# The even mixer takes RWKV's value columns before the attention's columns

## The chip, the cores and the metric

One Trainium2 chip, one of its cores. The metric is the device time of one launch in microseconds (us). All numbers before the result come from the kernel before the change: three timed runs and one profiled execution. The engines are called PE (TensorE), ACT (ScalarE), DVE (VectorE), POOL (GpSimd) and SP (the queue that loads the weights).

## What is computed

A trunk of two layers over 256 tokens of 1024 features, in float32. Each layer is a macaron: a half-step SwiGLU FFN, a mixer, a second half-step FFN, each with an RMSNorm before and after. The change touches only the mixer of layer 0, the "even" one, which runs two things side by side on the same normed input `h`:

```python
z = h @ w_in                                   # 1536 attention + 1792 RWKV columns
qa, ka, va = split(za)                         # differential attention, 4 heads, 2 x 64 / 128
r, k, v, xw, xa, xg = split(token_shift(zb))   # RWKV-7, 8 heads of 64
oa = softmax(q1 k1) va - lam * softmax(q2 k2) va
state = state * w + (state @ -kk) (kk a) + v k ;  y = state @ r      # token by token
mix = concat(rms_norm(oa), group_norm(y) * g) @ w_out
```

The order in which the columns of `w_in` are multiplied does not matter for the result.

## The kernel before, in words

The 256 tokens are two blocks of 128. All weights stream from HBM once as units of 128 x 2048 values, each loaded in two halves by SP's queue (line 289), and split by ACT (line 299) and DVE (line 300) into two float32r parts. A product with streamed weights is three passes: lines 315 to 317 (`proj`, tokens on the partitions, 12 products of 512 columns a unit and block), lines 340 to 342 (`proj_features`, features on the partitions, both blocks at once, 48 products of 256 columns a unit) and lines 327 to 329 (`outp`, output products, 12 a unit and block). The text calls all of these the wide products. At most 4 units are held split, counted from the slower block (`NW`, line 281).

The even mixer has 17 units: 13 of inputs and 4 of outputs. `EVEN_ORDER` (line 45) says in which order the inputs come: k, r, low-rank, q2, k2, v2 (attention's value), v (RWKV's value). k, r, v2 and v are two units each, q2 and k2 are two units of two heads each, low is one. The function that uses a finished input (`left`, line 859) is called one unit later, for the low-rank inputs and the last entry of the order at once.

Three further lines of work hang on them:

- `low_rank` (line 746) forms RWKV's features and puts `rwkv` (line 1059) of its block on a lane (2 x block). Its steps, each up to a `yield`: `pl`, `pt`, five doublings of the inverse (lines 1107, 1114), `pm` and `po` (lines 1128, 1133); then it waits for RWKV's value (lines 1139, 1140) and, in block 1, for block 0's state (line 1144); then `pr` and `pz` twice (lines 1155 to 1164), in block 0 the state (lines 1173 to 1184), two steps of `pk` and `py` (lines 1192, 1197 to 1200), and the norm with `pg` (line 1222).
- `value` (line 780) forms RWKV's value: scaled by ACT, mixed with the token before by DVE and `pv` on PE (line 785, in block 1 also line 787).
- `attention` (line 935) is put on lane 1 once q2 and k2 are there, block 0 ahead of block 1: scores `sp` (line 950), softmax on DVE and ACT (lines 953 to 972), transposes and weighted sums `op` (lines 983, 989) once v2 is there, norm and two turns (line 349). Block 0 does its four heads at once, block 1 two and two.

The order is set by a planner, `run` (line 1252). Block 0 may be `LAG` = 3 units ahead of block 1, in the units that `LAGS` names only 2. After every unit each lane takes a step (lane 2 slightly more), and when no block can go on, lanes take steps alone:

```python
order = (0, 1) if ready(0) else (1,) if ready(1) else ()
if not order:
    waits = [False, False]
    order = (0, 1) if ready(0) else (1,) if ready(1) else ()
    self.step_lanes()
```

Lanes issue with a lift in priority (`LIFT`, 200 for lane 0, 600 for lanes 1 and 2). From that the framework fixes each engine's order of instructions ahead of time. Transposes, scores, sums and `pv` share two PSUM banks (`tp`).

After the inputs `even` takes four output units, attention's two first and then RWKV's two (line 875); block 0's wait until both blocks are through with the inputs, block 1's until block 0's recurrence is done.

Of the kernel before, what the change touches and what calls it, by code (L numbers as in the profile page):

```python
# [15 lines left out]
PSUM = bass.MemoryType.PSUM  # L16

P = 128
# [7 lines left out]
LAM_INIT = 0.2  # L26
NW = 8  # half units, split
NRAW = 3  # half units, as loaded
LAG = 3
LAG0 = (6, 12)  # L30
WIDE = 16
LAGS = {"even": (7, 10, 2)}
LIFT_PRE, LIFT_POST = 300, 100
# [6 lines left out]

# units of the weight stream, and where each sub-layer starts
U_FFN, U_EVEN, U_ODD = 3 * NCH, 17, 32
# columns of the even mixer's inputs in the order that they are taken: RWKV's k, r, v and
# low-rank inputs, the attention's q2, k2, v2
EVEN_ORDER = ("k", "r", "low", "q2", "k2", "v2", "v")
PLAN = [("ffn", 0, 0), ("even", 0, 0), ("ffn", 0, 1), ("ffn", 1, 0), ("odd", 1, 0), ("ffn", 1, 1)]
SIZES = {"ffn": U_FFN, "even": U_EVEN, "odd": U_ODD}


# ---------------------------------------------------------------- constants of the shapes  # L50
def _columns(spec):
# [13 lines left out]
CO, CO_N = _columns([("dec", 4 * 2 * 128)])  # L65
# per-feature parameters, one feature per partition
PR, PR_N = _columns(
# [45 lines left out]

# ---------------------------------------------------------------- layout of the inputs
def _layout(inputs):
    a = {n: np.asarray(v) for n, v in inputs.items()}
    f = np.float32

    def cols(w, k_tiles=4):
        # [K, n] -> units of k_tiles K-tiles of n columns each  # L120
        k, n = w.shape
        return w.reshape(-1, k_tiles, P, n).transpose(0, 2, 1, 3).reshape(-1, P, k_tiles * n)

    def ffn(l, j, i):
        c0, c1 = JOINT.get(i, JOINT[None])
        w = a["ffn_wgu"][l, j]
        # halves of the inputs with gate and up side by side, or all the inputs of gate and then of up
        solo = w.reshape(2, 4, P, 2, NCH, 256).transpose(4, 0, 2, 1, 3, 5).reshape(NCH, 2, P, 2048)
        both = w.reshape(8, P, 2, NCH, 256).transpose(3, 2, 1, 0, 4).reshape(NCH, 2, P, 2048)
        gu = np.concatenate([solo[:c0], both[c0:c1], solo[c1:]])  # L130
        dn = cols(a["ffn_wd"][l, j], 2)
        out = []
        for c in range(NCH):
            out += [gu[c, 0], gu[c, 1]]
            if c:
                out.append(dn[c - 1])
        return out + [dn[NCH - 1]]
# [33 lines left out]
    units = []  # L171
# [48 lines left out]

# ---------------------------------------------------------------- the kernel
class Trunk:
    def __init__(self, ctx, tc, io, out, plan):
# [13 lines left out]
        nc.scalar.dma_start(out=c0, in_=io["c0"])  # L237
        # what is loaded ahead of which half unit: (block, half of the features)
        self.ahead = {X[0]: [(0, 0)], X[1]: [(0, 1)], X[2]: [(1, 0), (1, 1)]}
        nc.vector.memset(self.mhalf, -0.5)  # L240
        # the parts of the inputs' transposes, [features, block, tokens]
        self.xh = self.sb.tile([P, 8, 2, P], F32R, name="xh")
# [4 lines left out]

        # weight stream
        self.n_units = sum(SIZES[s[0]] for s in plan)
        self.pos = [0, 0]  # L250
        self.raws, self.split, self.n_dma, self.n_split = {}, {}, 0, 0

    # -------- small helpers
    def col(self, name, i=0, rows=P):
# [13 lines left out]
    def ps(self, tag, name="ps"):  # L268
        # two banks for each tag: ac0, ac1 (sums of the blocks), mm, tp
        return self.ps_p.tile([P, 512], F32, tag=tag, name=name)  # L270
# [6 lines left out]

    # -------- weights: load, then split each value exactly into two float32r parts
    def pump(self):
# [23 lines left out]

    # -------- products with the streamed weights (three exact-part passes)
    def proj(self, ps, u, first, last, xT, width=512):
# [25 lines left out]
    def proj_features(self, ps, u):  # L331
        # [2 x 128 features, 256 tokens], of both blocks
        w, xh, xl = self.split[u], self.xh, self.xl
# [10 lines left out]
    def turn(self, b, src, g=None):  # L344
        # [128 tokens, 2, 128] -> parts of its transpose, scaled by feature
        nc = self.nc
# [14 lines left out]

    # -------- norms
    def power(self, v, eps, n=1, name="rs"):
        # (v + eps) ** -0.5
        s = self.small(n, "pw_in")
        r = self.small(n, name, bufs=6)
        self.nc.vector.tensor_scalar(out=s, in0=v, scalar1=eps, scalar2=None, op0=ALU.add)
        self.nc.gpsimd.tensor_tensor(out=r, in0=s, in1=self.mhalf[:, :n], op=ALU.pow)
        return r

    def power2(self, v, eps, name):
        # (v[0] + v[1] + eps) ** -0.5
        s = self.small(1, "ssv")
# [39 lines left out]
    def spread(self, b, rs):  # L413
        # 1 / rms of the inputs along the free dimension
        rw = self.t2("rw")[:, :P]
# [36 lines left out]

    # -------- SwiGLU
    def ffn(self, b, u, l, j):
        """Hidden features 256 at a time: the first and the last ones block by block, the others for both
        blocks at once, whose products come out with the features on the partitions, as the second
        product takes them."""
        nc = self.nc
# [80 lines left out]

    # -------- retention  # L540
    def odd(self, b, u, l, j):
        """The queries and keys come out with the features on the partitions, for both blocks at once
        and without the norm's factors: the keys' go with the values, the queries' with the head's norm."""
        nc, mx, S = self.nc, self.mix, self.shared
# [124 lines left out]

    # -------- differential attention and RWKV-7 side by side  # L670
    def even(self, b, u, l, j):
# [21 lines left out]
        def last_cols(parts):  # L693
            # columns of equal height together
            at = 0
# [7 lines left out]
        def shifted(parts, name):  # L703
            # parts: (source [p, 128] in PSUM, mu, 1 - mu, destination, slot)
            zm = T2("zm", 516).rearrange("p (a t) -> p a t", a=4)
# [87 lines left out]

        # of both blocks at once, two heads at a time, [features, block, tokens]; the norm's factors
        # go with the keys here and with the scores for the queries
        def keys(i, ps):
# [72 lines left out]

        # the sums take banks that the other block is through with  # L870
        def free():
# [18 lines left out]
    def even_setup(self):  # L890
# [9 lines left out]
        self.row(S["muv"], R_MUV, 512, nc.sync)  # L900
        # 1 - mu, and the two coefficients of 1 + (a - 1) k_a in terms of tanh
        om = mx.tile([P, 20], F32, name="om")
# [14 lines left out]
        S["sub"] = sub  # L917
        # -lambda on every partition
        lv = self.t2("lv")[:, :256]
# [15 lines left out]
    def attention(self, b, qT, kT, rs):  # L935
        nc, mx, S = self.nc, self.mix, self.shared
        V, A, mm = nc.vector, nc.scalar, nc.tensor.matmul
        n, H = (b + 1) * P, 4 >> b  # keys, and heads at a time
        d0 = CE["dist"][0] + 256 - n
# [63 lines left out]
    def rwkv_features(self, b, fk, fr, th, ta):  # L1003
        """What the recurrence needs of each feature, in the scale of the block's middle."""
        nc, mx, S = self.nc, self.mix, self.shared
# [9 lines left out]
        for g in range(2):  # L1015
# [28 lines left out]
            A.activation(out=kk, in_=kk, func=AF.Square)  # L1044
            # the first two columns of each product count; more cost nothing, and the array's clock
            # does not fall for want of work
            pn = self.tp("pn")[:, : 8 * WIDE].rearrange("p (n i c) -> p n i c", n=2, i=2)
# [11 lines left out]
    def rwkv(self, b, F, sxg):  # L1059
# [7 lines left out]
        else:  # L1067
            # the features of the block are formed: their room serves the recurrence
            ln, nt, xx, yy, pp = (mx.tile([P, 8, 64], F32, tag=t, name="work") for t in ("th", "ta", "fk", "fr", "w"))
        h8 = lambda ap: ap.rearrange("p (h c) -> p h c", c=64)  # L1070
        # two banks, one for each row half of the array: even heads and odd heads
        pair = lambda name, n: [ac(name)[:, : 4 * n].rearrange("p (h c) -> p h c", h=4) for _ in range(2)]
# [7 lines left out]

        # triangular system inside each half block
        pl = pair("pl", 64)
# [16 lines left out]

        # inverse of the system, by doubling the solved blocks  # L1100
        groups = (slice(0, 4), slice(4, 8))
# [35 lines left out]

        # state that the block starts from, in the block's own scale, head by head
        while f"v{b}" not in S:
# [28 lines left out]
        if not b:  # L1168
            # state after the block
            st = mx.tile([P, 4, 64], F32, tag="st", name="st")  # L1170
# [32 lines left out]

        # norm over each head, bonus, gate
        lw, lb = self.t2("lnw"), self.t2("lnb")
# [20 lines left out]

    # -------- run
    def block(self, b):
# [105 lines left out]
```

## Time and profile before

| what | us |
|---|---|
| median of the three timed runs | 1209.59 |
| lowest and highest run | 1209.18, 1213.92 |
| span of the profiled execution, first to last instruction | 1225.8 |
| another time of that execution | none is given beside its span |
| PE busy in it | 1201.0 (98%) |
| DVE busy, ACT busy | 690.7 (56%), 576.1 (47%) |
| mean granted clock of TensorE | 0.979 |

A profile shows one execution, from the first to the last instruction. Busy time of PE is modelled, as matmuls are pipelined, so a full PE is not PE at its peak. The granted clock is a share of the full speed; 0.50 is the lower of two levels (1.2 GHz against 2.4). A float32 product shows as two instructions. An instruction's row gives its start, its length, engine, line, operation, output and inputs, its shape, how many like it follow (x4), and in brackets how long the engine idled before it and what ended that.

### The profile page before, as it was taken

Reading aid. Unit: us, or ns where it says so; the run is one execution under the profiler, and the core shown is the slowest. Engines: PE = TensorE matmul, PEld = TensorE weight load, DVE = VectorE, ACT = ScalarE, POOL = GpSimd, SP = SyncE. Lnnn points to the kernel's source line nnn. Section 1 sums busy time; section 2 is a strip of 40 time slices with the busy share of each in tenths; the row PEclk is TensorE's granted clock in tenths of the full one; section 3 lists DMA queues with packets and bytes.
Section 4 is the critical chain, followed back from the end, with each engine's and each line's share of the span. In section 5 each row is a group of like instructions: output and inputs, shape, how many; then the busy total and the mean of one; then the engine's idle time right before and its main releaser. Section 6 shows DMA issues by size and latency. Waiting matters only on the chain.

```text
span 1225.8 us, 19872 instructions
## 1 busy us (share of the span) xinstructions
PE 1201.0 (98%) x8072; PEld 1050.6 (86%) x8072; DVE 690.7 (56%) x987; ACT 576.1 (47%) x895; POOL 38.9 (3%) x53
## 2 busy tenths in 40 slices
PE   7999999999999999999999999999999999999997
PEld 6999997888778769999978999988987777899996
DVE  5664456787552475554565555565445557555453
ACT  6554446743541264444465444456434456544442
POOL 0000001000011100000010000000000001000000
PEclk9999999999995799999999999999999999999999
DMA  8665556431230056555555655555525555555651
GB/s 277 219 224 176 190 178 192 138 105 61 68 114 1 31 165 214 190 175 188 181 181 172 198 180 194 182 181 191 190 85 180 163 167 188 182 196 184 196 185 39
DMA packets 55419, 199.84 MB, mean 163 GB/s; under 512 B 6176, under 2 KB 6432, under 8 KB 55328
## 3 DMA queue, kind: packets, MB, share of 16 engines
q1 hardware_dynamic: 54576, 196.90, 49.2%
q8 instruction: 63, 1.03, 0.3%
q0 software_dynamic: 320, 1.05, 0.3%
q10 hardware_dynamic: 432, 0.63, 0.2%
q14 instruction: 28, 0.23, 0.1%
HBM read 197.50 MB, written 1.05 MB: 162 GB/s over the span
## 4 chain that ended last, share of the span: by engine, by line
PE 87%; DVE 3%; ACT 3%; DMA 3%; issue 2%; POOL 1%; SPq 0%; DVEq 0%; POOLq 0%; ACTq 0%
PE ps L340 13%; PE ps L342 13%; PE ps L341 13%; PE ps L328 8%; PE ps L327 8%; PE ps L329 8%; PE ps L315 4%; PE ps L317 4%; PE ps L316 4%; DMA raw<-in_wts_dram 2%; ACT wh L299 1%; DVE wl L300 1%; PE pk L1192 1%; PE p L1107 1%; PE p L1114 1%
## 5 line engine op out<-in xcount | busy, mean ns | idle before, releaser
L300 DVE TENSOR_TENSOR wl<-raw,wh 128x1024 fp32r<-128x1024 f32 (+1 forms) x368 | 442.5, 1205 | 378.2 <-ACT wh L299 375.5
L299 ACT CAST wh<-raw 128x1024 fp32r<-128x1024 f32 (+1 forms) x368 | 379.3, 1035 | 446.1 <-PE ps L341 275.7
L340 PE MATMUL ps<-xh,wh 128*128 128x256 f32 x1376 | 390.9, 284 | 1.8 <-DVE sgh L491 1.4
L342 PE MATMUL ps<-xh,wl 128*128 128x256 f32 x1376 | 390.1, 284 | 0.0
L341 PE MATMUL ps<-xl,wh 128*128 128x256 f32 x1376 | 389.4, 283 | 0.0
L340 PEld LDWEIGHTS ps<-xh,wh 128*128 128x128 f32 x1376 | 263.5, 192 | 6.3 <-DVE sgh L491 2.3
L341 PEld LDWEIGHTS ps<-xl,wh 128*128 128x128 f32 x1376 | 263.5, 192 | 1.6
L342 PEld LDWEIGHTS ps<-xh,wl 128*128 128x128 f32 x1376 | 263.6, 192 | 0.5
L328 PE MATMUL ps<-wl,hx 128*128 128x512 f32 x448 | 180.2, 402 | 0.0
L327 PE MATMUL ps<-wh,hx 128*128 128x512 f32 x448 | 178.5, 399 | 0.0
L329 PE MATMUL ps<-wh,hx 128*128 128x512 f32 x448 | 178.1, 398 | 0.0
L315 PE MATMUL ps<-wh,xh 128*128 128x512 f32 (+1 forms) x320 | 129.8, 408 | 2.2 <-ACT xh L401 1.6
L316 PE MATMUL ps<-wl,xh 128*128 128x512 f32 (+1 forms) x320 | 126.6, 398 | 0.0
L317 PE MATMUL ps<-wh,xl 128*128 128x512 f32 (+1 forms) x320 | 125.3, 396 | 0.7 <-DVE xl L402 0.7
L329 PEld LDWEIGHTS ps<-wh,hx 128*128 128x128 f32 x448 | 84.8, 189 | 20.3 <-issue 0.5
L327 PEld LDWEIGHTS ps<-wh,hx 128*128 128x128 f32 x448 | 85.0, 190 | 19.9 <-issue 0.5
L328 PEld LDWEIGHTS ps<-wl,hx 128*128 128x128 f32 x448 | 84.8, 189 | 17.6
L315 PEld LDWEIGHTS ps<-wh,xh 128*128 128x128 f32 x320 | 60.7, 190 | 21.7 <-ACT xh L401 6.7
L317 PEld LDWEIGHTS ps<-wh,xl 128*128 128x128 f32 x320 | 60.6, 189 | 15.5 <-DVE xl L402 2.7
L316 PEld LDWEIGHTS ps<-wl,xh 128*128 128x128 f32 x320 | 60.6, 189 | 12.7 <-issue 1.7
L401 ACT ACTIVATE xh<-tp,c 128x128 fp32r<-128x128 f32 x96 | 32.3, 366 | 11.0 <-PE tp L396 6.5
L402 DVE SCALAR_TENSOR_TENSOR xl<-tp,c,xh 128x128 fp32r<-128x128 f32 x96 | 30.7, 347 | 11.9 <-ACT xh L401 10.3
(233 smaller groups left out, 831.0 us busy)
## 6 DMA issues: line engine op xcount, KB each, us to landing
raw<-in_wts_dram SPq DMA_DIRECT2D x362, 512.0 KB, 4.5
gpost<-in_rows_dram SPq DMA_DIRECT2D x6, 512.0 KB, 5.6
x<-in_x_dram SPq DMA_DIRECT2D x4, 256.0 KB, 6.1
ups<-in_ups_dram SPq DMA_DIRECT2D x1, 768.0 KB, 7.4
ce<-in_ce_dram SPq DMA_DIRECT2D x1, 644.0 KB, 7.3
lnw<-in_rows_dram POOLq DMA_DIRECT2D x2, 256.0 KB, 4.0
lnb<-in_rows_dram POOLq DMA_DIRECT2D x2, 256.0 KB, 3.6
dec<-in_co_dram SPq DMA_DIRECT2D x1, 512.0 KB, 3.4
```

Source lines behind the costliest of these rows:

```text
L299: nc.scalar.copy(out=h[:, c], in_=r[:, c])
L300: nc.vector.tensor_tensor(out=l[:, c], in0=r[:, c], in1=h[:, c].bitcast(F32), op=ALU.subtract)
L315: mm(ps[:, :width], lhsT=xh[:, kt, :], rhs=h[:, c], start=first and i == 0, stop=False)
L316: mm(ps[:, :width], lhsT=xh[:, kt, :], rhs=l[:, c], start=False, stop=False)
L317: mm(ps[:, :width], lhsT=xl[:, kt, :], rhs=h[:, c], start=False, stop=last and i == n - 1)
L327: mm(acc[n], lhsT=hh[:, t], rhs=wh[:, c], start=first and t == 0, stop=False)
L328: mm(acc[n], lhsT=hh[:, t], rhs=wl[:, c], start=False, stop=False)
L329: mm(acc[n], lhsT=hl[:, t], rhs=wh[:, c], start=False, stop=last and t == 1)
L340: mm(o, lhsT=h[:, c], rhs=xh[:, kt], start=kt == 0, stop=False)
L341: mm(o, lhsT=h[:, c], rhs=xl[:, kt], start=False, stop=False)
L342: mm(o, lhsT=l[:, c], rhs=xh[:, kt], start=False, stop=kt == 7)
L401: nc.scalar.mul(out=xh[:, kt, :], in_=t, mul=g)
```

## The change

RWKV's value columns are taken right after the low-rank inputs, before q2, k2 and v2, so that v2 is now the last of the inputs. The host lays out the weights in the same order (line 143). The stretch in which block 0 may be only two units ahead moves by two units with the joint products. The other lines of the diff take out comments.

```diff
-LAGS = {"even": (7, 10, 2)}
+LAGS = {"even": (9, 12, 2)}
...
-EVEN_ORDER = ("k", "r", "low", "q2", "k2", "v2", "v")
+EVEN_ORDER = ("k", "r", "low", "v", "q2", "k2", "v2")
```

## Rows read from the trace of the kernel before

**Rows 1.** The page's 40 slices: granted clock in tenths of full speed.
```profile
PEclk9999999999995799999999999999999999999999
```

**Rows 2.** Busy time by stretch: stretch, length, engines' busy us (x instructions), clock, DMA share, GB/s.
```profile
364.00:368.00 4.00, 4.00 (x36) 3.27 (x34) 1.03 (x3) 3.29 (x11) 0.00 (x0) 0.95 0.00 0
...
412.00:416.00 4.00, 4.00 (x10) 2.52 (x10) 2.60 (x5) 1.00 (x2) 0.00 (x0) 0.57 0.00 0
```

**Rows 3.** The same table for longer stretches (PE, PEld, DVE, ACT, POOL, clock).
```profile
230.00:335.00 105.00, 103.81 (x1262) 86.37 (x1261) 78.38 (x181) 51.93 (x125) 4.87 (x6) 1.00 0.29 92
...
349.00:367.60 18.60, 18.16 (x156) 13.95 (x154) 11.03 (x18) 8.53 (x23) 3.79 (x5) 1.00 0.41 134
367.60:415.40 47.80, 47.80 (x203) 39.02 (x202) 12.87 (x24) 6.27 (x17) 4.98 (x4) 0.50 0.00 1
```

**Rows 4.** The same table for line 327 alone (PE, PEld, clock, DMA, GB/s).
```profile
349.00:367.60 18.60, 0.88 (x2) 0.32 (x2) 1.00 0.41 134
367.60:412.90 45.30, 2.03 (x3) 1.00 (x3) 0.50 0.00 1
```

**Rows 5.** PE in order of time: the recurrence and RWKV's value.
```profile
277.03 0.68 PE L1133 MATMUL po<-ar,be 64*64 64x64 f32 x16
...
330.30 1.12 PE L785 MATMUL pv<-zv,ce 128*128 128x512 f32 x2
...
334.93 1.03 PE L1155 MATMUL pr<-rv,gram 128*64 128x64 f32 x14
...
355.99 1.12 PE L785 MATMUL pv<-zv,ce 128*128 128x512 f32 x2
357.05 1.12 PE L787 MATMUL pv<-ups,ce 32*128 32x512 f32 x2
```

**Rows 6.** PE in order of time: last key product, attention's scores and turns.
```profile
301.71 0.28 PE L342 MATMUL ps<-xh,wl 128*128 128x256 f32 x1
...
303.10 0.72 PE L950 MATMUL sp<-akT,hx 64*128 64x128 f32 x8
...
333.09 0.38 PE L349 MATMUL tp<-c,hx 128*128 128x128 f32 x2
...
333.87 1.13 PE L950 MATMUL sp<-akT,hx 64*128 64x256 f32 x4
...
395.89 1.12 PE L349 MATMUL tp<-c,hx 128*128 128x128 f32 x4
```

**Rows 7.** PE in order of time: two wide products in a row.
```profile
426.20 0.40 PE L329 MATMUL ps<-wh,hx 128*128 128x512 f32 x1
426.43 0.39 PE L327 MATMUL ps<-wh,hx 128*128 128x512 f32 x1
```

**Rows 8.** Groups of instructions, 225 to 430 us: count, busy us, mean ns, idle before.
```profile
L963 ACT ACTIVATE s<-s,mx 128x128 f32<-128x128 f32 (+1 forms) x16 | 7.1, 442 | 12.0 <-DVE mx L959 12.0
...
L953 DVE SCALAR_TENSOR_TENSOR s<-sp,rs,ce 128x512 f32<-128x512 f32 x6 | 4.4, 748 | 1.5 <-PE sp L950 0.9 <-PE pk L1192 0.7
...
L957 DVE TENSOR_REDUCE mx<-s 128x4 f32<-128x1024 f32 (+1 forms) x3 | 3.6, 1212 | 0.0
...
L971 ACT ACTIVATE s<-s,ri 128x128 f32<-128x128 f32 (+1 forms) x8 | 3.1, 445 | 1.8 <-DVE ri L969 1.7
L963 ACT ACTIVATION_READ_ACCUMULATOR s<-s,mx 128x1 f32 x16 | 3.0, 187 | 0.0
L972 DVE SCALAR_TENSOR_TENSOR s<-s,ri 128x128 f32<-128x128 f32 (+1 forms) x8 | 3.0, 412 | 1.3 <-ACT s L971 1.3
```

**Rows 9.** ACT's waits, 349 to 428 us: total us, times, longest.
```profile
ACT pT L985 <- PE tp L983: 12.2, 1, 12.2
```

**Rows 10.** Groups on PE, 349 to 428.4 us: the output products.
```profile
L329 PE MATMUL ps<-wh,hx 128*128 128x512 f32 x23 | 11.3, 498 | 0.0
L328 PE MATMUL ps<-wl,hx 128*128 128x512 f32 x24 | 10.8, 452 | 0.0
L327 PE MATMUL ps<-wh,hx 128*128 128x512 f32 x24 | 10.8, 448 | 0.0
```

## The prediction

> **What bounds the kernel now.** I read the page's slices first, then narrower stretches of the same table, then PE's instructions in order of time, and last the attention's own instructions. The slices show one place in the whole span where the granted clock is not full: [rows 1] has one slice at 5 and the next at 7. The stretch table dates it: it starts just inside the stretch at 0.95 and ends inside the one at 0.57 [rows 2]; 367.6 to 415.4 us holds it entirely, 47.80 us at 0.50, which is the lower of TensorE's two levels (1.2 GHz instead of 2.4), and PE is busy for all 47.80 us of it [rows 3]. So the even mixer's tail is not waiting for something: PE works through it at half speed. The same work at the full clock takes 47.8 / 2 = 23.9 us, and 23.9 us is what a tail without the dip would give back.
>
> What did PE do before the clock fell? From 349 to 367.6 us it was busy for 18.16 of 18.60 us [rows 3], so it did not idle. But of the wide products with streamed weights only two of line 327 lie there, and three in the 45 us after it [rows 4]; all else is the small float32 work of the recurrence and the attention. The clock came back after the wide output products had set in at 412.9. Why is the small work bunched there? Block 0's recurrence runs its triangular part to 277.03 and then has no step for 57.9 us: its next product, `pr` of line 1155, starts at 334.93, some 4.6 us after `pv` of line 785 at 330.30, the product that makes block 0's value [rows 5]. Lines 1139 and 1140 are that wait. Block 1's recurrence needs block 0's state, so it is held too. Everything after `pr`, for both blocks, falls behind the last input projection.
>
> **The change, part by part.** *Order.* Value's columns go from units 11 and 12 to units 5 and 6. Units, sizes, the count of products, the weight loads (same number and size on SP's queue, only the host's order differs) and their splitting on ACT and DVE stay the same. Cost of the order itself: zero instructions added, zero removed. What each value step issues moves with it: per block one scaling on ACT, two passes on DVE, `pv` on PE at 1.12 us, and for block 1 a second product of 1.12 [rows 5]. They go to a stretch where DVE is busy 78.38 of 105 us [rows 3]; I cost that move at nothing as PE has the query and key products to do meanwhile; with that cover gone it is at most the 3 x 1.12 = 3.4 us of PE once over, which PE pays today anyway.
>
> *Lag.* The stretch in which block 0 may run only 2 units ahead moves from units 7 to 9 to units 9 to 11. Both times it begins at the second half of the joint products; it adds no work. I cost it at nothing.
>
> *What is earlier.* Walking the planner by hand (which block is ready, which lane gets a step after each unit): before, block 0's `pr` is issued after unit 12 of block 0; after the change it comes after the second query unit, and block 0's state is formed before the last key unit. Block 1's recurrence then waits for no value, and its last step comes beside the last attention-value units. So the recurrence lies among wide products instead of behind them. Gain: up to 23.9 us, the dip.
>
> *What is later.* The attention. Its scores need the keys, and those are now behind value. Before, the last key product is at 301.71 [rows 6]. In front of it now go 48 wide products of value at 0.23 apart [rows 7] = 11.0 us, the three `pv` products of 3.4, and the part of block 0's recurrence up to its state, which took 334.93 to 355.99 = 21.1 [rows 5]. Lower end 301.7 + 14.4 = 316, upper end 301.7 + 14.4 + 21.1 = 337; I take 337, as the planner issues all of it ahead of the last key unit. Block 0's attention took 303.10 to about 333.5, 30.4 us from scores to its second turn [rows 6]: 337 + 30.4 = 368. Block 1's attention follows in the same lane. It took 333.87 to 397.0, 63.1 us [rows 6]. That is the upper end; 28.3 us of it lay in the half clock (367.6 to 395.9), so at the full clock it is 63.1 - 14.2 = 49. One softmax half by its own instructions: scores 2 x 1.13, two 0.75, one 1.21, four exponentials of 0.44 with a read of 0.19, two pairs of about 0.45 and 0.41 [rows 6, 8] = 9.2 us; with transposes, sums, norm and turn I estimate 26 for two halves. Lower end 26, upper 49 (63 if nothing improves). In between I take 35, nearer the lower: ACT alone waited 12.2 us for one transpose that stood behind recurrence products in PE's order [rows 9], and in the new order the recurrence is through by then. So block 1's attention ends at 368 + 35 = 403.
>
> *Does PE run dry before that?* By 428.4 the old kernel has done 24 + 24 + 23 = 71 of the 96 output products [rows 10]; at the full clock that is 428.4 - 23.9 = 404.5. In the new order the 48 output products of block 1 cannot start before 403. Against the old order's 25 left these are 23 more, 23 x 0.23 = 5.3 us, so PE has other work until 404.5 - 5.3 = 399.2. The next layer can't fill in: the weight window reaches 4 units past the slower block. PE idles 403 - 399.2 = 3.8 us.
>
> **Sum.** 23.9 - 3.8 = 20.1 us off a span of 1225.8. The profile gives a span and no other time for its execution; the median of the runs is 1209.59, 16.2 less. I take the 20.1 off the median: 1189.5. With 26 for block 1's attention there is no idle and the time is 1185.7; with 49 it is 403 + 14 - 399.2 = 17.8 idle, so 1203.5.
>
> **A rule against the trace.** [Rows 3] show the clock falling with PE 98% busy and no gap behind it. The Trainium skill's page "TensorE: Matmul & The Clock Gate", section "Why this matters for your kernels", has it that idle gaps in PE bring the half rate back; here the fall needed no gap, so a busy PE alone is no safety. By that rule the 3.8 us hole in front of block 1's output products would bring a second, short dip.
>
> **The rivals.**
> - *The hole drops the clock.* PE waits 3.8 us for block 1's attention and the output products start at 1.2 GHz. The first wide products before ran slow from 412.9 to 415.4 [rows 2, 3, 4], 2.5 us, half of it lost: 1.2; with the small attention work in the hole at half speed some 2 more: 1193. Against it: the hole may not exist.
> - *Attention becomes the bound (slower).* Block 1's attention keeps its 63 us, because its transposes and sums still queue behind other work in PE's fixed order. Then it ends at 368 + 63 = 431, PE idles 431 - 399.2 = 31.8 us, and the sum is 31.8 - 23.9 = 7.9 us slower: 1217.5. It decides from an end past 399.2 + 23.9 = 423. For it: PE's order is fixed ahead and both blocks share two banks for scores, transposes and sums. Against it: the 12.2 us wait and the dip are part of those 63 us.
> - *The dip moves.* Both recurrences now run at once with a lift over the wide products; if they crowd these out of 285 to 335, the clock falls there instead and 47.8 us at half rate stay: 1209.6, within 6. For it: DVE is busy 75% there and will slow the chains [rows 3]. Against it: the planner puts a unit of wide products between every two steps.
> - *The change doesn't do what it says in the timed runs.* They are 16.2 us below the span; if that were a shorter dip, only 23.9 - 16.2 - 3.8 = 3.9 us are to be had: 1205.7.
>
> **How the numbers follow.** Forecast 0.64; hole with low clock 0.08; dip moved 0.11; shorter dip 0.04; attention bound 0.13. About 0.5%, 6 us, is what a measurement of this kernel can tell from no change. Forecast and hole are faster: 0.72. The dip moved or shorter: 0.15 the same. The attention bound is slower: 0.13. The range starts at 1184, just below the no-idle 1185.7, and reaches over the moved dip to 1213; most of the attention case and a little at the bottom are left out. The forecast's own range is 1185.7 to 1203.5.
>
> **What would show it.** Right: no slice under full clock around 370 to 415; `pr` of block 0 before the last key product; the last `pg` of line 1222 before the last projection; PE's waits list an attention turn ahead of line 327, a few us. Wrong: a dip of the same length anywhere, or a PE gap of over 20 us behind attention.

## The result, and the profile after

The changed kernel takes 1227.72 us (median of 4 runs, 1226.37 to 1228.44), the kernel before in the same comparison 1209.38 (4 runs, 1208.66 to 1213.92): 1.0127 times as long, 95% interval 1.0094 to 1.0159 (the medians alone give 1.0152, inside that interval). By the medians it is 18.3 us slower where 20.1 us less were forecast, outside the range. All ratios in this text leave out those runs of the kernel before that were over 1.5% above its fastest, 13 of 48 in the experiments, so the quotient of two medians can differ from them.

To read what follows one number has to be known first. The profile of before in [rows 1 to 4] was not like the runs that it was set beside. The kernel before, profiled a second time (the first experiment below), had this, in the page's busy line and its slices:

```profile
PE 1183.5 (98%) x8072; PEld 1035.6 (86%) x8072; DVE 690.6 (57%) x987; ACT 575.9 (48%) x895; POOL 38.9 (3%) x53
PEclk9999999999989999999999999999999999999999
```

and the changed kernel this:

```profile
span 1226.0 us, 19883 instructions
PE 1188.6 (97%) x8072; PEld 1040.7 (85%) x8072; DVE 691.5 (56%) x987; ACT 576.0 (47%) x895; POOL 39.4 (3%) x53
PEclk9999999999998999999999999999999999999999
```

Neither has the deep dip of [rows 1]. The span of the second profile of before is 1210.4 us, so PE idles 1210.4 - 1183.5 = 26.9 us in it; in the changed kernel 1226.0 - 1188.6 = 37.4 us. That is **10.5 us more idle time**, and 5.1 us more busy time for the same 8072 instructions. Where? The stretch table of the changed kernel, then that of before (second profile); columns are the stretch, its length, then busy time of PE, PEld, DVE, ACT and POOL, the granted clock, DMA share, GB/s:

```profile
360.00:380.00 20.00, 20.00 (x114) 17.04 (x113) 9.05 (x15) 7.23 (x24) 0.00 (x0) 0.91 0.16 54
380.00:400.00 20.00, 14.35 (x51) 10.07 (x50) 13.20 (x23) 10.88 (x30) 2.66 (x2) 0.74 0.31 105
400.00:420.00 20.00, 14.53 (x71) 10.90 (x71) 8.44 (x19) 9.54 (x31) 1.01 (x1) 0.97 0.00 1
420.00:440.00 20.00, 18.48 (x74) 14.19 (x74) 11.00 (x22) 10.41 (x21) 1.12 (x2) 0.86 0.41 132
```

```profile
360.00:380.00 20.00, 19.56 (x176) 15.16 (x174) 10.54 (x18) 4.47 (x15) 2.30 (x2) 1.00 0.21 62
380.00:400.00 20.00, 20.00 (x143) 16.62 (x142) 10.67 (x20) 5.24 (x14) 4.99 (x4) 1.00 0.00 1
400.00:420.00 20.00, 18.59 (x85) 13.32 (x84) 15.05 (x30) 10.69 (x26) 2.75 (x3) 1.00 0.32 105
420.00:440.00 20.00, 19.07 (x85) 14.38 (x85) 12.74 (x25) 13.51 (x27) 2.01 (x2) 1.00 0.58 178
```

Of these 80 us PE is busy for 67.36 in the changed kernel and for 77.22 before: 9.9 of the 10.5 us lie here, in the mixer's tail, nearly all from 380 to 420. The clock column has the other part: below full in all four stretches, and full in before's. What does PE wait for? Its waits from 360 to 440 us (what waits, what ended it, total us, times, longest):

```profile
PE tp L349 <- DVE hx L998: 8.6, 2, 5.3
...
PE op L989 <- ACT pT L985: 1.4, 2, 0.7
```

Line 998 is the scaling by the norm at the end of the attention, and `tp` of line 349 its turn for the output products. Both blocks' attentions are waited for. PE in order of time shows how it came to that (start, length, what, in brackets the idle time before):

```profile
285.75 0.56 PE L1155 MATMUL pr<-rv,gram 128*64 128x64 f32 x6
...
336.77 0.33 PE L1155 MATMUL pr<-rv,gram 128*64 128x64 f32 x2
...
362.90 1.71 PE L1222 MATMUL pg<-ups,sxg 128*128 128x512 f32 x2
...
369.46 0.28 PE L342 MATMUL ps<-xh,wl 128*128 128x256 f32 x1
371.97 0.71 PE L950 MATMUL sp<-akT,hx 64*128 64x128 f32 x8
...
382.17 1.16 PE L989 MATMUL op<-av,pT 128*128 128x128 f32 x8
388.65 1.09 PE L349 MATMUL tp<-c,hx 128*128 128x128 f32 x4 [5.33 <-DVE hx L998]
...
391.71 2.46 PE L950 MATMUL sp<-akT,hx 64*128 64x256 f32 x8 [0.19 <-DVE hx L357]
...
402.28 1.16 PE L989 MATMUL op<-av,pT 128*128 128x128 f32 x8 [0.68 <-ACT pT L985]
...
413.73 1.16 PE L989 MATMUL op<-av,pT 128*128 128x128 f32 x8 [0.68 <-ACT pT L985]
418.13 0.63 PE L349 MATMUL tp<-c,hx 128*128 128x128 f32 x4 [3.24 <-DVE hx L998]
```

Read it beside [rows 5, 6]. Block 0's recurrence goes on at 285.75 instead of 334.93, so the change does what it was said to do. Block 1's recurrence follows at 336.77; its `pg` is done at 364.6 and its last `py` at 366.4, all of it ahead of the last key product, which came at 301.71 before and now comes at 369.46. So the attention of both blocks is the last thing in the mixer. It is a chain of small steps, and the output products wait for it: block 0's for 5.33 us, block 1's for 3.24. The wait of [rows 9], an attention copy on ACT behind recurrence products, is down from 12.2 us to 1.2 at the longest, as forecast; it did not matter.

The granted clock around the two holes, in short stretches cut where PE stops and starts (columns as above):

```profile
384.00:388.00 4.00, 0.00 (x0) 0.00 (x0) 1.88 (x5) 3.38 (x11) 1.26 (x2) 1.00 0.75 265
388.00:398.40 10.40, 9.43 (x25) 6.59 (x26) 7.80 (x12) 2.40 (x9) 1.40 (x1) 0.51 0.28 97
398.40:415.00 16.60, 14.60 (x72) 10.97 (x70) 5.90 (x14) 7.49 (x25) 0.00 (x0) 1.00 0.00 1
415.00:418.00 3.00, 0.00 (x0) 0.00 (x0) 0.88 (x3) 2.31 (x9) 1.01 (x1) 1.00 0.00 0
418.00:423.00 5.00, 4.53 (x15) 3.52 (x16) 3.44 (x7) 0.94 (x3) 0.56 (x1) 0.66 0.01 2
```

Each hole is followed by a stretch at the lower level (1.2 GHz): 10.4 us at 0.51 behind the first, part of 5 us at 0.66 behind the second. When the output products could start, they started slow.

**A measure that takes the clock out.** For every execution a span and a mean granted clock are known. Span times clock is an estimate of the time that the execution would have taken at the full clock throughout; it counts every slow stretch as if PE alone set the pace in it. The kernel before ran 48 times beside the experiments: its time went from 1204.87 us (clock 0.998) to 1233.22 (0.976), but span times clock stayed at 1202.0 us on average, with a standard deviation of 1.5. The changed kernel's first four executions have 1213.2. (A run's time is about 1.8 us over its span.) So the 18.3 us come apart: 1213.2 - 1202.0 = **11.2 us without the clock**, close to the 10.5 us of idle time; and to the clock the medians lose 1227.7 - 1.8 - 1213.2 = 12.7 us against 1209.4 - 1.8 - 1202.0 = 5.6, that is **7.1 us more**. The first part repeats below (1212.7 in after_again, 1212.5 in order_alone), the second does not: by span x (1 - clock) the 48 executions of the kernel before lost 14.1 us to the clock on average (half of them under 12.2, 13 of them 24.5 or more), and the changed kernel's eight lost 14.9. So by this measure the change costs some 11 us; that it also costs something through the clock is not shown.

### The profile page after: what moved, and what is told of

It is laid out like the page before. It is cut to its first block, busy times and chain, and to the rows that moved or that the text cites. A ratio compares the mean times of both kernels' runs of the same rounds, so it can differ in the third digit from the quotient of the medians.

```text
span 1226.0 us, 19883 instructions
## 1 busy us (share of the span) xinstructions
PE 1188.6 (97%) x8072; PEld 1040.7 (85%) x8072; DVE 691.5 (56%) x987; ACT 576.0 (47%) x895; POOL 39.4 (3%) x53
## 4 chain that ended last, share of the span: by engine, by line
PE 82%; DVE 5%; DMA 5%; ACT 4%; issue 3%; POOL 1%; SPq 0%; DVEq 0%; POOLq 0%; ACTq 0%
PE ps L340 13%; PE ps L342 13%; PE ps L341 13%; PE ps L328 7%; PE ps L329 7%; PE ps L327 7%; PE ps L317 4%; PE ps L315 4%; DMA raw<-in_wts_dram 4%; PE ps L316 4%; ACT wh L299 2%; DVE wl L300 2%; PE p L1107 1%; PE p L1114 1%; PE pk L1192 1%
## 5 line engine op out<-in xcount | busy, mean ns | idle before, releaser
L402 DVE SCALAR_TENSOR_TENSOR xl<-tp,c,xh 128x128 fp32r<-128x128 f32 x96 | 30.4, 346 | 11.7 <-ACT xh L401 10.7
```

## The experiments

All times are us; "full clock" is span times clock, the mean over the kernel's executions; PE's idle time is that of the profiled execution. The ratio is to the kernel before on the same chip.

| kernel | median | ratio (95%) | full clock | PE idle |
|---|---|---|---|---|
| before_again | 1215.88 | 1.0039 (0.9958 to 1.0119) | 1204.3 | 26.9 |
| lag_alone | 1212.91 | 1.0014 (0.9970 to 1.0058) | 1205.6 | 24.3 |
| order_alone | 1231.47 | 1.0167 (1.0124 to 1.0210) | 1212.5 | 35.2 |
| v_before_v2 | 1223.52 | 1.0102 (1.0057 to 1.0146) | 1203.4 | 27.3 |
| q2_v_k2 | 1216.40 | 1.0017 (0.9980 to 1.0054) | 1209.2 | 29.4 |
| core_out_first | 1231.12 | 1.0150 (1.0105 to 1.0195) | 1211.4 | 36.3 |
| core1_no_lift | 1277.00 | 1.0392 (1.0234 to 1.0550) | 1229.9 | 28.8 |
| lifts_none | 1306.41 | 1.0631 (1.0458 to 1.0805) | 1243.9 | 26.1 |
| after_no_norm | 1211.57 | 0.9973 (0.9936 to 1.0011) | 1200.6 | 30.2 |
| before_no_norm | 1203.75 | 0.9928 (0.9896 to 0.9960) | 1194.9 | 24.9 |
| after_halves | 1227.48 | 1.0156 (1.0081 to 1.0231) | 1210.0 | 33.5 |
| q2_v_k2_halves | 1211.70 | 1.0024 (0.9982 to 1.0067) | 1208.0 | 28.1 |
| after_again | 1230.96 | 1.0143 (1.0083 to 1.0204) | 1212.7 | 38.3 |
| fill_wide | 1234.35 | 1.0159 (1.0094 to 1.0224) | 1216.3 | 33.9 |
| fill_f32 | 1232.07 | 1.0150 (1.0079 to 1.0221) | 1217.4 | 37.5 |

### Was the profiled execution a usual one?

The kernel before, unchanged (before_again).

> The kernel before, unchanged. Theory A (the profile that the prediction used was not typical: in the timed runs the stretch at 1.2 GHz is shorter): time 1209, span about 1208, half clock for under 20 us, as 47.8 us would cost 23.9. Theory B (the profile was typical): span about 1226 and again some 48 us at half clock.

Measured: a span of 1210.4 us at a clock of 0.996, 15.4 us shorter than the first profile, as theory A had it. It loses (1 - 0.996) x 1210.4 = 4.8 us to the clock, where the first profile's clock of 0.979 lost (1 - 0.979) x 1225.8 = 25.7. Full clock, the two are 1205.6 and 1200.1. So the dip on which the forecast rested belonged to that execution and not to the timed runs beside it, in which there were some 5 us to win and not 24. It is not a rarity either: 13 of the 48 later executions have a clock of 0.980 or less, like the first profile's 0.979. What a dip can give back is a matter of many runs, and neither of these two profiles is the usual one.

### Order or lag?

The diff has two lines; each alone. order_alone is the changed kernel with the old lag, lag_alone the kernel before with the new one.

```diff
 # order_alone
-LAGS = {"even": (9, 12, 2)}
+LAGS = {"even": (7, 10, 2)}
 # lag_alone
-LAGS = {"even": (7, 10, 2)}
+LAGS = {"even": (9, 12, 2)}
```

> Value's columns early as in the change, but the two-unit lag where it was (units 7 to 9). Theory A (the attention, now last, is the loss): within 4 us of the changed kernel's 1227.7. Rival (the shifted lag holds block 0 back): back to 1215 or less.

> The old order of the columns, the lag moved to units 9 to 11. Theory A: 1209 within 4 us. Rival (the lag is the loss): 1218 or more.

Measured: the order alone has the whole loss (1.0167, idle 35.2 us, full clock 1212.5), the lag alone none that can be told (1.0014). The order it is.

### Which part of the order?

Two orders in between: value ahead of v2 only, and value between the query and the key columns.

```diff
-EVEN_ORDER = ("k", "r", "low", "v", "q2", "k2", "v2")
+EVEN_ORDER = ("k", "r", "low", "q2", "k2", "v", "v2")   # v_before_v2, LAGS (7, 10, 2)
+EVEN_ORDER = ("k", "r", "low", "q2", "v", "k2", "v2")   # q2_v_k2, LAGS (9, 12, 2)
```

> Order k, r, low, q2, k2, v, v2: keys as early as before the change, RWKV's value ahead of the attention's value only. Theory A (late keys put both attentions at the end of the sub-layer with nothing beside them): no hole behind block 0's turn, 1200 to 1211. Rival (any earlier recurrence uses up the cover that the tail needs): 1216 or more.

> Order k, r, low, q2, v, k2, v2 with the changed kernel's lag. Theory A (what counts is how late the keys are): as the changed kernel, 1222 to 1231. Rival (what counts is that value is early): 1215 or less.

Measured for v_before_v2: 1.0102, which the first theory had excluded. Its stretches of the tail:

```profile
380.00:420.00 40.00, 38.37 (x195) 31.50 (x194) 17.29 (x32) 12.22 (x35) 4.95 (x4) 0.74 0.01 2
```

PE does not run dry here (27.3 us idle in all, as before), but this stretch has a clock of 0.74, with PE 38.37 of 40 us busy. At full clock the kernel is at 1203.4, level with before. So the two losses can come apart: this execution pays nothing in idle time and 16 us to the clock ((1 - 0.987) x 1220.6). The order has two executions only (0.987 and 0.983), and the kernel before has clocks from 0.975 to 0.999, so that the order lowers the clock is not shown.

q2_v_k2 came out level with before (1.0017) at 1216.40 us, between what the two theories said. With the query columns ahead of value, they no longer stand between value and the keys, and the last key product is earlier. PE's product of line 342, 230 to 430 us (count, shortest, median and longest ns, first and last start), in q2_v_k2 and in the changed kernel:

```profile
L342 PE MATMUL ps<-xh,wl x64: 277/283/683, 235.6 to 346.2; 128*128 128x256 f32 x64
```

```profile
L342 PE MATMUL ps<-xh,wl x64: 278/283/679, 256.0 to 369.5; 128*128 128x256 f32 x64
```

The keys are 23 us earlier and the idle time is 29.4 instead of 37.4 us, 8 of the 10.5 us. So with the keys earlier most of the idle time is back. At full clock it is less: 1209.2 against 1213.2 is 4.0 of the 11.2 us. The kernel is level in time by the clocks of its eight executions (0.991 to 0.998); what the other 7.2 us over before are, beyond 2.5 us of idle time, is open.

### Can other work fill the holes?

RWKV's two output units first, the attention's last, so that PE has the finished recurrence's output products to do while it waits.

```diff
-        return out + list(cols(a["even_w_out"][0], 2))
+        wo = list(cols(a["even_w_out"][0], 2))
+        return out + wo[2:] + wo[:2]
...
-        for i, job in enumerate((att, att, core, core)):
+        for i, job in enumerate((core, core, att, att)):
```

> The changed kernel with the output units in the order RWKV, RWKV, attention, attention (the host's order too; RWKV's turned parts lie in the room of its own features). Theory A (PE runs dry because the output products stand behind the attention, which is now last): RWKV's 48 output products fill the holes, PE's idle time falls from 37.4 us to under 30, 1214 to 1220. Rival (the loss is the clock, or the recurrence): within 4 us of 1227.7.

Measured: 1.0150, idle 36.3 us: nothing gained. PE in order of time shows why:

```profile
381.50 1.16 PE L991 MATMUL op<-av,pT 128*128 128x128 f32 x8
387.98 1.09 PE L350 MATMUL tp<-c,hx 128*128 128x128 f32 x4 [5.32 <-DVE hx L1000]
391.04 2.46 PE L952 MATMUL sp<-akT,hx 64*128 64x256 f32 x8 [1.97 <-DVE hx L358]
394.14 0.69 PE L350 MATMUL tp<-c,work 128*128 128x128 f32 x2 [0.64 <-DVE s L955]
395.29 0.79 PE L328 MATMUL ps<-wh,hr 128*128 128x512 f32 x1 [0.46 <-ACT hr L354]
```

The turn of the recurrence (`tp` from `work`) stands behind block 0's attention turn and behind block 1's scores in PE's order, which is fixed ahead of time, with the attention lifted. The first hole stays as it was, another of 1.97 us is new, and only the last hole of 3.24 is gone, with one of 1.64 behind block 1's softmax in its place. The work was there, and its place in the order was not.

### Are the recurrence's lifts what puts it ahead?

The changed kernel without the lift of block 1's lane, and of both recurrences' lanes.

```diff
-LIFT = (200, 600, 600)
+LIFT = (200, 600, 0)    # core1_no_lift
+LIFT = (0, 600, 0)      # lifts_none
```

> The changed kernel with block 1's recurrence alone not lifted (LIFT 200, 600, 0). Theory A: keys earlier and some of block 1's recurrence beside the attention, 1213 to 1222. Rival: 1225 or more.

> The changed kernel without the lift of the two recurrences (LIFT 0, 600, 0; the attention keeps its own). Theory A (the lifted recurrence of block 1 pushes the last key product to 369 us): the last key product before 350, PE's idle time under 31 us, 1210 to 1219. Rival (without the lift the recurrences end the sub-layer): 1224 or more.

Measured: both far slower, 1.0392 and 1.0631, a plain miss. The last key product came not earlier but later, at 399.5 and 423.6 us against 369.5, so taking the lift away does not bring the keys forward. The idle time did fall (28.8 and 26.1 us, the level of before). The clock did not hold. In lifts_none:

```profile
300.00:340.00 40.00, 40.00 (x228) 28.84 (x226) 10.83 (x17) 5.70 (x11) 0.00 (x0) 0.65 0.15 47
340.00:380.00 40.00, 40.00 (x253) 28.10 (x249) 12.12 (x24) 2.95 (x4) 0.55 (x1) 0.57 0.09 29
380.00:420.00 40.00, 40.00 (x178) 27.88 (x179) 4.88 (x9) 2.12 (x4) 2.82 (x3) 0.53 0.07 24
```

120 us in which PE shows no idle time, at little more than half the clock. So a full busy column is no sign of a full clock, as [rows 3] had it already. By the measure above the clock explains (1 - 0.949) x 1309.1 = 67 us of the profiled execution; at full clock the kernel still is some 42 us over before, without more idle time. What those are was not found out.

### What do the holes cost? Leaving the norm out

The norm over each head at the end of the attention is left out (squares, power, scaling), in the changed kernel and in the kernel before, so that the turn follows the copy directly.

```diff
-        ss = self.small(4, "ss4", 2)
...
-            for i, h in enumerate(heads):
-                self.sumsq(op[:, i * P : (i + 1) * P], P ** -0.5, ss[:, h : h + 1])
             yield
-        r4 = self.power(ss, EPS, 4, "r4")
-        V.tensor_tensor(out=ma, in0=ma, in1=r4[:, :, None].to_broadcast([P, 4, P]), op=ALU.mult)
         yield
```

> Left out: the attention's norm over each head (squares, power, scaling) in both blocks; all else is the changed kernel. Theory A (the loss is idle time of PE at the end of the attention's chain, plus some half clock): in the changed kernel's trace PE waits 5.33 us and 3.24 us for the scaling of that norm, and from the last sum to the turn it is 383.33 to 388.65 and 414.9 to 418.13; without the norm the turn can follow the copy, at 384.2 and 415.3. So 4.5 + 2.8 = 7.3 us less than the changed kernel: ratio to before near 1.007 instead of 1.0127. Rival B (the holes cost nothing, since the next stretch waits for weights or for the clock anyway): at most 2 us less, ratio 1.011 or more.

> Left out: the same norm, from the kernel before. Theory A: there the attention of both blocks ends beside other work, and PE had no wait over 1 us in the mixer, so the same cut brings 1.5 us at most: ratio 0.9985 to 1.000. Rival B (the cut brings what the work itself costs on ACT and DVE, wherever it stands): as much as in the changed kernel.

Measured: 0.9973 and 0.9928. PE's waits from 360 to 440 us in after_no_norm:

```profile
PE tp L982 <- DVE s L971: 3.1, 3, 1.4
PE op L988 <- ACT pT L984: 2.0, 3, 0.7
PE tp L349 <- ACT hx L992: 0.7, 1, 0.7
```

The 8.6 us in front of line 349 have become 0.7, and the idle time fell from 37.4 to 30.2 us: 7.2, where the rows gave 7.3. Both expected ratios were too high, since the cut had a side effect: in both kernels the FFN's feature products, which have nothing to do with the mixer, became shorter. The values that go on are others; that this is the reason was not tried. The group of line 340 from 440 us on, before_again, then before_no_norm (in the changed kernel it goes from 284 to 281 ns):

```profile
L340 PE MATMUL ps<-xh,wh 128*128 128x256 f32 x992 | 281.3, 284 | 1.4 <-ACT q L634 1.1 <-DVE q L632 0.3
```

```profile
L340 PE MATMUL ps<-xh,wh 128*128 128x256 f32 x992 | 278.2, 280 | 1.6 <-ACT q L634 1.3 <-DVE q L632 0.3
```

Both kernels have it, so it about drops out of the comparison of one with the other. At full clock the cut takes 1213.2 - 1200.6 = 12.6 us off the changed kernel and 1202.0 - 1194.9 = 7.1 off the kernel before: 5.5 us more in the changed one. The idle time says the same: it falls by 7.2 us in the changed kernel and by 2.0 in the kernel before (26.9 to 24.9), 5.2 more. In the medians the changed kernel is 1211.57 against 1203.75, a gap of 7.8 us instead of 18.3; of these 1200.6 - 1194.9 = 5.7 are left at full clock, beside 30.2 - 24.9 = 5.3 us of idle time. The three waits shown are about that remainder: PE now waits for the attention's softmax and copies, and before_no_norm has none of these waits from 360 to 440 us. The one fall that after_no_norm's profile has in the mixer is not behind a hole. This is the experiment that shows the loss: shorten the last chain and PE's idle time goes, in the kernel where that chain is last, and the time at full clock goes by as much. It accounts for half of the 11.2 us; the other half stands beside idle time that remains, in the waits shown.

### A shorter chain without leaving anything out

Block 1's attention takes its heads two and two, one pair behind the other. Here the second pair's scores and softmax are issued ahead of the first pair's sums; the second tile takes the room of `ar0`.

```diff
-            s = mx.tile([P, 2, H, n], F32, tag="s", name="s")
+            s = mx.tile([P, 2, H, n], F32, tag="s" if not h0 else "ar0", name="s")
+            kept.append(s)    # kept = [] ahead of the loop
...
-            while f"av{b}" not in S:
-                yield
+        while f"av{b}" not in S:
+            yield
+        for h0, s in zip(range(0, 4, H), kept):
+            heads = range(h0, h0 + H)
```

> The changed kernel, with the scores and softmax of block 1's second pair of heads issued ahead of the sums of its first pair (its tile takes the room of block 0's ar, which is free by then). Theory A: the chain 391.7 to 418.1 loses most of the second softmax (403.4 to 412.45, 9 us) and ends ahead of the output products that cover it; the holes of 3.24 and 0.68 us behind it go, 4 to 5 us off: ratio near 1.009. Rival B: no less than 1.0115.

> The order k, r, low, q2, v, k2, v2 (ratio 1.0017 before) with the same reordering of block 1's attention. Theory A: its trace has one hole of 3.2 us behind the attention's norm and 4.4 us idle in 400 to 420; 3 us less: ratio 0.9975 to 1.000, so level with the kernel before or just under it. Rival B: unchanged, 1.0017 or more.

Measured for after_halves: 1.0156, no gain in time. The idle time fell by 3.9 us (37.4 to 33.5) and the full clock time by 3.2 (1213.2 to 1210.0), near the 4 to 5 us expected, but the ratio is on the rival's side. Its four executions have clocks of 0.982 to 0.992, the changed kernel's eight 0.981 to 0.991, so a gain of this size is under what the clock does from run to run; that the clock took it is not shown. q2_v_k2_halves has 1.0024, level with before, and at full clock it gained 1.2 us (1209.2 to 1208.0) where 3 were expected; its profiled execution has a span of 1209.6 at a clock of 0.999 and no slice under full. None of the orders beats the kernel before: the best of them at full clock, v_before_v2, is not below 1202.0.

### Do the holes make the clock fall?

after_again is the changed kernel once more. The other two put products that nobody reads behind the last sums of each block's attention, to fill the holes: wide products of the projections' form, or float32 ones.

```diff
+            if h0 + H == 4:
+                idle = self.tp("idle")
+                for k in range((20, 12)[b]):    # fill_wide
+                    mm(idle, lhsT=self.xh[:, 0, 0], rhs=self.xh[:, 0:2].rearrange("p a b t -> p (a b t)"), start=True, stop=True)
+                for k in range((4, 2)[b]):      # fill_f32
+                    mm(idle, lhsT=self.ident, rhs=S["av0"], start=True, stop=True)
```

> The changed kernel unchanged, beside the two below on one chip. Its first profile: span 1226.0, PE idle 37.4 us, 20.5 us at half clock, three of the four falls right behind a hole of PE. Both theories: 1.010 to 1.016 against before; idle between 35 and 39 us, since the holes come from waits that every execution has, and half clock between 14 and 31 us.

> The changed kernel, with products that nobody reads put on PE behind the last sum of each block's attention, where the two holes are: 20 wide products for block 0, 12 for block 1, of the same form as the projections' (0.23 us each: 4.6 and 2.8 us). Nothing is left out. Theory G (the clock falls because of the holes): the holes are filled, the turns start when they did, and the three falls behind them (10.2, 3.4, 3.4 us) are gone: 17 / 2 = 8.5 us less than the changed kernel, ratio to it 0.993. Theory S (the clock falls because small float32 work stands without wide products, holes or not): the falls stay, and the time is the changed kernel's or up to 2 us more.

> The same with float32 products of 512 columns in the holes, 4 for block 0 and 2 for block 1 (1.12 us each: 4.5 and 2.2 us). Theory G: as with the wide ones, about 8 us less than the changed kernel. Theory S, with float32 as what the clock can't stand: the falls stay or grow, no gain. If the wide ones gain and these don't, the kind of product decides and not the gap alone.

after_again repeats the changed kernel: the same two holes, and a clock of 0.52 from 389.9 to 400.3 us, again from about the moment PE starts after the first (390.2). In fill_wide the filler stands from 394.16 to 399.0; the stretches around it:

```profile
394.00:399.00 5.00, 4.99 (x24) 3.81 (x22) 2.71 (x5) 4.46 (x13) 1.18 (x2) 1.00 0.65 218
399.00:408.00 9.00, 7.04 (x32) 5.24 (x33) 7.69 (x12) 0.92 (x3) 1.47 (x1) 1.00 0.33 113
408.00:413.00 5.00, 1.91 (x10) 0.99 (x8) 1.22 (x4) 3.46 (x11) 0.00 (x0) 1.00 0.02 3
413.00:423.60 10.60, 10.05 (x30) 7.56 (x31) 3.55 (x6) 3.75 (x16) 0.00 (x0) 0.52 0.00 0
```

fill_f32 has the same picture some 9 us earlier:

```profile
390.50:400.00 9.50, 8.03 (x36) 5.83 (x36) 7.19 (x12) 1.92 (x7) 0.97 (x1) 1.00 0.26 96
400.00:404.40 4.40, 1.22 (x6) 0.71 (x6) 1.22 (x4) 2.49 (x8) 0.00 (x0) 0.97 0.00 0
404.40:414.80 10.40, 9.94 (x30) 7.38 (x30) 3.64 (x7) 3.83 (x15) 0.00 (x0) 0.52 0.01 2
```

With the first hole filled (all but 0.74 us of it in fill_wide, all but 1.88 in fill_f32), the clock holds through the 9 us behind it, with wide and with float32 filler alike. Then it falls behind the next thin stretch: 1.91 us busy of 5 in fill_wide, 1.22 of 4.4 in fill_f32, both in block 1's softmax, and the low stretch is as long as before. The two falls of 3.4 us behind the later holes are gone in both: the clock is 1.00 from 423.6 to 450 us in fill_wide and from 414.8 to 445 in fill_f32, and 0.84 from 418 to 440 in the changed kernel and in after_again. So theory G is right about where the clock falls, and its forecast of 8.5 us was wrong: the long fall moves to the next hole. Why is there a next hole? PE in order of time in fill_wide:

```profile
402.78 1.52 PE L950 MATMUL sp<-akT,hx 64*128 64x256 f32 x8 [0.89 <-DVE hx L357]
...
411.67 0.63 PE L983 MATMUL tp<-c,s 128*128 128x128 f32 x3 [2.50 <-DVE s L972]
...
413.08 2.08 PE L989 MATMUL op<-av,pT 128*128 128x128 f32 x8 [0.68 <-ACT pT L985]
```

From block 1's first scores to its first sums are 413.08 - 402.78 = 10.3 us at the full clock, and PE waits 2.50 us for the softmax on the way. In the changed kernel it is 402.28 - 391.71 = 10.6 us, most of it at half clock, and PE does not wait: the slow output products fill the time that the softmax takes on DVE and ACT. From block 0's turn to these scores it is 3.1 us in both (388.65 to 391.71, 399.73 to 402.78). So the long fall behind the first hole cost this chain some 0.3 us and not half of its length, and taking it away uncovers a wait. The time went up by nothing that can be told (1.0159 and 1.0150 against 1.0143), though at full clock the fillers cost 3.6 and 4.7 us against after_again. Theory S is not excluded as a second cause. In v_before_v2 the clock falls at 331 us with no hole ahead of it:

```profile
321.00:331.00 10.00, 10.00 (x78) 7.10 (x76) 2.60 (x3) 2.21 (x3) 0.00 (x0) 1.00 0.14 47
331.00:342.00 11.00, 11.00 (x60) 8.05 (x59) 1.92 (x2) 2.80 (x4) 1.05 (x1) 0.53 0.18 54
```

## Why the prediction was wrong

- **"The same work at the full clock takes 47.8 / 2 = 23.9 us": the first step that failed, by its size.** The dip was read rightly from its rows, but they show one execution. The timed runs did not have it: 1225.8 us of span would be a run of 1227.6, 18 us over the median of 1209.59, and that difference stood in the text. The 20.1 us were then taken off a median that did not hold them; those runs had some 5 us to give. As to the dip, the rival "shorter dip", at 4 in 100, was the case. (A detail beside it: [rows 4] count one of the three lines of the output products. With all lines six wide products lie ahead of the dip and ten in it, still few.)
- **Order and lag cost nothing of themselves:** right as far as added work goes. Value's steps found cover, and the lag alone changes nothing.
- **What is earlier:** right. `pr` of block 0 comes at 285.75, ahead of the last key product, and the last `pg` (362.90) ahead of the last projection.
- **"Lower end 316, upper end 337; I take 337": the second step that failed.** The last key product came at 369.46. The bound counted block 0's recurrence up to its state and stopped there; whatever else now goes ahead of the keys it put at nothing. Once that state exists, block 1's recurrence can run too: it lies from 336.77 to 366.4, with some 40 wide products of lines 340 to 342 between its own. The rest of block 0's recurrence (`pk` to `pg`) and block 1's triangular part went ahead as well: of the 640 products of lines 1107 and 1114, 464 had started before the last key product in the old order, and all of them in the new. Together these make up about the 32.5 us that are missing.
- **Block 0's attention, 30.4 us:** 17.8 measured, from the scores at 371.97 to the turn's end at 389.74. **Block 1's, "in between I take 35":** 27.1 (391.71 to 418.8), near the lower end of 26 that the single instructions gave. So the chain's length was over-estimated twice, its start was put 32.5 us too early, and its end came at 418.8, not 403. The two errors in length took about half of the error in the start back, which is luck.
- **"PE idles 3.8 us":** 10.5 more than before. The sum looked at one hole only, ahead of block 1's output products. The larger one, 5.33 us, stands ahead of block 0's, which wait for block 0's attention in the same way; that attention now ends with nothing beside it.
- **The slower rival, "attention becomes the bound":** this is what happened, at 13 in 100. Its price was 7.9 us slower and its deciding point an end past 423. Both were built on the 23.9. With some 5 us to win in its place the point is 399.2 + 5 = 404, and the measured 418.8 lies 15 us past it. The mark of 399.2 was off too: by it PE would idle 418.8 - 399.2 = 19.6 us, and it idled 10.5 more than before.
- **The rival "the hole drops the clock":** its mechanism is in the trace, with a longer stretch than it had: 10.4 us at half clock behind the first hole. Its price is another matter, since the chain behind that hole lost only some 0.3 us by it. The Trainium skill's page "TensorE: Matmul & The Clock Gate", section "Why this matters for your kernels", has it that idle gaps of PE bring the half rate back; the trace agrees for these holes (0.51 from 388.0 to 398.4 right behind 5.33 us of idle time), and fill_wide and fill_f32 agree, where the fall leaves the filled hole. [Rows 3] and lifts_none show that it is not the only way.
- **The signs:** three of the four signs of being right came true (`pr`, `pg`, the wait of an attention turn) and neither sign of being wrong, and the kernel was slower. None of them gave a time for the last key product, on which the rest hung.

Shown by experiment: that the order and not the lag is the loss; that idle time of PE at the end of the attention's chain is the loss at full clock, half of it by taking the norm out; that the long fall of the clock stands behind the first hole and leaves it when it is filled. Not shown: that the falls behind the holes make the changed kernel slower, since the kernel before loses as much to the clock over many runs. Open: why the clock also falls where PE shows no hole.

## What to carry to other kernels

Before a slow clock in a profile is priced, set the profile's span beside the timed runs: if they are shorter by about as much as the dip costs, they do not have it, and it can't be taken off them. Span times mean clock compares two kernels without it, and here it told 11 us apart with a standard deviation of 1.5, where the times themselves spread over 28. It says nothing on what one slow stretch costs: where another engine sets the pace, slow products can fill what would be a wait.

Moving one chain early moves another late. Ask which chain is the last one afterwards, follow everything that the earlier one now lets start ahead of it (here the other block's recurrence), and price the last chain by its length at the end, where nothing lies beside it.

## What the runs showed of the hardware

- The same program on the same kind of chip differed by 28 us in 48 executions (1204.87 to 1233.22), nearly all of it in the granted clock (0.999 to 0.975).
- PE was busy for 40.00 of 40 us in three stretches in a row at clocks of 0.65, 0.57 and 0.53 (lifts_none).
- Behind the first hole (5.0 to 5.3 us) the clock was at the lower level for some 10 us in the changed kernel (0.51), in after_again (0.52), and in order_alone, core_out_first and after_halves (0.50). Filling the hole with products that nobody needs moved this stretch to the next hole and saved no time.
- 10.6 us of block 1's attention, most of them at half clock, took 10.3 at the full clock in fill_wide: the softmax on DVE and ACT set the pace, and PE's slow products filled a wait.
- With the norm left out, feature products far from the mixer went from 284 to 280 ns on average (line 340; to 281 in the changed kernel), at a clock of 1.00. Why was not tried.
